# RWKV recurrence round four PSUM banks, and half of the first output columns projected beside it

## The chip, the cores and the metric

One core of a Trainium2 chip runs the whole program in one launch. The metric is device time in microseconds (us). TensorE (PE, with its weight loads PEld) multiplies, VectorE (DVE), ScalarE (ACT) and GpSimd (POOL) do the elementwise work, and SyncE's queue (SP) issues nearly all transfers. TensorE writes its results into PSUM, of which the program holds eight tiles of 128x512 fp32 at a time, called banks below.

## The reference

Two transformer blocks on a sequence of 512 tokens of width 1024 in fp32: the first has a hybrid token mixer, a cross attention on a memory of 256 tokens and a gated feed-forward, the second three attention branches. The change lies in the mixer of the first block, which joins an mLSTM (512 columns) with an RWKV-7 recurrence (512 columns) and projects both with one matrix:

```
hm = mlstm_chunkwise(q, k, v, i_pre, f_pre)             # 4 heads of 128
y_m = sigmoid(o) * standardize_heads(hm) * m_norm_g     # columns 0 to 511

def step(state, inp):                                   # RWKV: 8 heads of 64, 512 steps
    r_t, w_t, k_t, v_t, kk_t, a_t = inp
    sk = einsum('bhvk,bhk->bhv', state, kk_t)
    state = (state * w_t[:, :, None, :]
             - sk[..., None] * (kk_t * a_t)[:, :, None, :]
             + v_t[..., None] * k_t[:, :, None, :])
    y = einsum('bhvk,bhk->bhv', state, r_t)
yr = standardize_heads(yr) * r_gn_g + r_gn_b + (sum(rr * kr * r_rk) * vr)
y_r = yr * g                                            # columns 512 to 1023

x = x + concatenate([y_m, y_r], -1) @ w_out             # 1024 x 1024
```

## The kernel before

Activations lie transposed, features on partitions and the 512 tokens along a row. A dense product of fp32 precision is three matmuls for each 128x128 weight tile: high part of the weight by high part of the input, high by low, low by high. `unit` loads 128x512 fp32 of weights (`wraw`), ScalarE rounds it to the high part (`whi`), VectorE subtracts to get the low part (`wlo`); three buffers hold each of the two. One tile of one weight unit, three matmuls of 128x512, is called a unit step below.

The stage around the change is a merge of two streams that is written out as generators. `woven` advances the stream whose fraction of work done is smaller; `steps(n, ...)` counts a stream's yields in n-ths. The first stream is `rwkv_chain`: the recurrence in eight groups g of 64 tokens, each with two chunks of 32. For each group it does

- `columns(g)`: transposes of `BK` and of the values `xT` into two banks, evacuated into `St` (ScalarE) and `Z` (ScalarE, VectorE);
- `sides(g)`: transposes of `KR`, and products of `Z` and `Gm`, two banks, evacuated into `rgu`;
- `solve(g)`: `rgu` by the inverse `TT`, one bank, evacuated into `Z`;
- `ops(g)`: products of `St` and `Z`, two banks, which VectorE adds to `DR` and writes to `St` (four instructions);
- `step(g, c)`, c = 0 and 1: the recurrence itself, `Z` by `St`, two banks, which give the next `Z` and a piece of the output, in `sg` or `yt`.

`columns` and `sides` run two groups ahead of `step`, `solve` and `ops` one. After each second group, `rwkv_out` takes a block of 128 tokens through group normalisation (VectorE), transposes, gain and bias (ScalarE) and the gate into `xT[:, 4:8]`; it makes its yields between those of the chain. The second stream is `mlstm`, with the heads' projections (into the banks `mm`), their attention (into the banks `q`) and at the end `mem_kv`, the keys and values of the cross attention. The order of TensorE's instructions is the program order of this merge (`PIN`); those of the other engines are ordered by a scheduler with priorities, weights first.

After the merge `mixer_out` multiplies by `w_out` in two halves of the contraction: q = 0 takes the mLSTM's four tiles of 128 features, split into high and low parts in the room of `KR`; q = 1 takes the RWKV's four, in the room of `Gm`. The first OE = 4 output tiles m open four banks (`early`) and do their half q = 0 first; then each m in turn is finished with its half q = 1, and `x` (in the room of `BK`) is transposed and added.

The eight banks are `mm` (2), `p` (2), `q` (2), `s` (1) and `y` (1). `pt()` without a tag takes the next of `self.turns`. In this stage `turns` is `["p"]`: every tile of `columns`, `sides`, `solve`, `ops` and `rwkv_out` goes to one of the two `p` banks, and `step` names `s` and `y`.

Of the kernel before, what the change touches and what calls it, by code (L numbers as in the profile page):

```python
# [9 lines left out]
F32R = mybir.dt.float32r  # L10
# [6 lines left out]
S = 512  # L17
D = 1024
NB = S // 128
# [10 lines left out]
PS, LS, CS, XS = 16, 75, 90, 188  # L30
RW = "tile"
GS = 31
OE = 4
MY = 2
# [42 lines left out]
def weave(*gens):  # L77
    for _ in woven(*gens):
        pass
# [20 lines left out]
class Build:  # L100
# [378 lines left out]
    def mixer(self, yT, hpool, kept):  # L479
        nc, i = self.nc, self.i  # L480
        hh, hl = self.halves()
        h = (hh, hl)
        tc = self.tc
        self.turns, self.mms = ["p", "q"], ["mm", "mm", "s"]
        with self.tc.tile_pool(name="st", bufs=1, reuse_waits=RW) as st:
            self.basics()
            vectors = self.vectors(st)
            next(vectors)
            self.start(st, yT, kept, hh, hl)
            next(vectors)  # L490
            self.masks(hpool, st)
        v = self.vec
        with tc.tile_pool(name="rk", bufs=1, reuse_waits=RW) as rk:
            KR = self.tile(rk, [128, 4, 8, 4, 32], "KR", 1)
            BK = self.tile(rk, [128, 4, 8, 4, 32], "BK", 1)
            VT = yT[:, 4:8, :]
            PC = rk.tile([128, 4, 16], F32, name="PC")
            xt = hpool.tile([128, 512], F32, name="xt")
            yt = hpool.tile([128, 512], F32, name="yt")
            nc.gpsimd.memset(yt, 0.0)  # L500
            Gm = self.tile(rk, [128, 2, 8, 4, 64], "Gm", 1)
            small = hpool.tile([128, 64], F32, name="rsmall")
            omu = self.omu = small[:, 0:15]
            self.ts(omu, v["r_mu"], -1.0, 1.0)
            w0h, a0h, kah, kah1 = (small[:, 16 + 4 * q:20 + 4 * q] for q in range(4))
            self.ts(w0h, v["r_w0"], 0.5)
            self.ts(a0h, v["r_a0"], 0.5)
            self.ts(kah, v["r_ka"], 0.5)
            self.ts(kah1, v["r_ka"], -0.5, 1.0)
            rk2 = small[:, 32:40].rearrange("p (j e) -> p j e", e=2)  # L510
            bonus = hpool.tile([128, 32], F32, name="bonus")
            for j in range(4):
                self.ts(rk2[:, j], self.hsel, v["r_rk"][:, j:j + 1])
            TT = hpool.tile([128, 32, 32], F32, name="TT")
            rwu = TT[:, 0:16].rearrange("p a b -> p (a b)")
            nc.gpsimd.dma_start(rwu[0:64], i["r_w_up"][0])
            nc.gpsimd.dma_start(rwu[64:128], i["r_a_up"][0])
            rgu = hpool.tile([128, 512], F32, name="rgu")
            nc.gpsimd.dma_start(rgu, i["r_g_up"][0, 0:128])
            nc.gpsimd.dma_start(xt[0:32], i["r_g_up"][0, 128:160])  # L520
            sg = hpool.tile([128, 512], F32, name="sg")
            gb = hpool.tile([128, 1], F32, name="gb")
            self.rw = dict(sg=sg, gb=gb, KR=KR, BK=BK, VT=VT, PC=PC, Gm=Gm, rk=rk, rgu=rgu, rwu=rwu, xt=xt, yt=yt, rk2=rk2, bonus=bonus)
            with tc.tile_pool(name="ml", bufs=1, reuse_waits=RW) as ml:
                lstm = self.mlstm(ml, h, yT, hpool, kept)
                with tc.tile_pool(name="prep", bufs=1, reuse_waits=RW) as pr:
                    self.rwkv_prep(pr, h, small)
                    for _ in part(lstm, PS):
                        pass
                self.turns, self.mms = ["p"], ["mm"]  # L530
                with tc.tile_pool(name="mid", bufs=1, reuse_waits=RW) as mid:
                    self.rw["G"] = mid.tile([128, 4, S], F32, name="G")
                    with tc.tile_pool(name="inv", bufs=1, reuse_waits=RW) as iv:
                        self.pinned = PIN[0]
                        gates = self.gates(ml, iv)
                        next(gates)
                        weave(self.rwkv_inv(iv, TT), steps(LS + 5, part(lstm, 12), gates, part(lstm, GS), self.gate_rows(iv),
                                                           part(lstm, LS - 12 - GS)))
                    with tc.tile_pool(name="chain", bufs=1, reuse_waits=RW) as ch:
                        self.pinned = PIN[1]  # L540
                        weave(steps(CS, self.rwkv_chain(ch, TT, yT)), steps(XS + MY - LS - PS, lstm))
                self.pinned = ""
                self.turns, self.mms = ["p"], ["mm", "mm", "q", "q"]
                self.mixer_out(yT, rk, ml)
# [172 lines left out]
    def rwkv_chain(self, ch, TT, yT):  # L717
# [3 lines left out]
        nc, R = self.nc, self.rw  # L721
# [101 lines left out]
        def step(g, c):  # L823
            z, st = made[g]
            ix = 2 * g + c
            yn = ys[ix // 4 % 2].rearrange("p (j e k) -> p j e k", j=4, e=2)
            qs = slice(32 * (ix % 4), 32 * (ix % 4) + 32)
            for q in range(2):
                p = self.pt("sy"[q])
                pv = p[0:96, 0:256].rearrange("p (j e k) -> p j e k", j=2, e=2)  # L830
                js = slice(2 * q, 2 * q + 2)
                for j in range(2):
                    for e in range(2):
                        self.mm(pv[:, j, e], st[c][:, 2 * q + j, e], z[c][:, 2 * q + j, e, 0:64])
                for dst, src in ([(Z[(ix + 1) // 2 % 2][1 - c][CS[c], js, :, 0:64], pv[0:64])] if ix < 15 else []) + [(yn[qs, js], pv[64:96])]:
                    if q:
                        nc.vector.tensor_copy(dst, src)
                    else:
                        self.act(dst, src)
# [3 lines left out]
        def main():  # L843

            def rest(n):
                for _ in range(n):
                    yield 0

            consts(0)
            columns(0)  # L850
            yield from rest(2)
            sides(0)
            yield from rest(2)
            solve(0)
            columns(1)
            yield from rest(2)
            ops(0)
            consts(1)
            sides(1)
            yield from rest(2)  # L860
            for g in range(8):
                step(g, 0)
                yield from rest(1)
                if g < 7:
                    solve(g + 1)
                yield from rest(2)
                step(g, 1)
                if g % 2:
                    lates.append(self.rwkv_out(ys[g // 2 % 2], g // 2, yT))
                yield from rest(1)  # L870
                if g < 7:
                    ops(g + 1)
                    yield from rest(2)
                if g < 6:
                    consts(g + 2)
                    columns(g + 2)
                    yield from rest(2)
                    sides(g + 2)
                    yield from rest(2)


# [362 lines left out]
                nc.sync.dma_start(kept["v"].rearrange("p (s d) -> p s d", s=2)[:, s2, cc], t)  # L1244


    def mixer_out(self, xT, rk, ml):
        nc, i = self.nc, self.i
        x = self.tile(rk, [128, NB, D], "BK", 1)
        y = [self.tile(rk, [128, 2, 4, S], tag, 1, F32R) for tag in ("KR", "Gm")]  # L1250
        for q in range(2):
            for k in range(4):
                self.split_from(y[q][:, 0, k], y[q][:, 1, k], xT[:, 4 * q + k])
            if q == 0:
                for b in range(NB):
                    nc.sync.dma_start(x[:, b], i["x"][0, 128 * b:128 * b + 128, :])

        def half(ps, m, q):
            wu = self.unit(i["w_out"][0][512 * q:512 * q + 512, 128 * m:128 * m + 128], 4, 128)
            self.dense(ps, wu, (y[q][:, 0], y[q][:, 1]), range(4), q == 0, q == 1)  # L1260

        early = [self.pm() for _ in range(OE)]
        for m, ps in enumerate(early):
            half(ps, m, 0)
        for m in range(KD):
            if m < OE:
                ps = early[m]
            else:
                ps = self.pm()
                half(ps, m, 0)  # L1270
            half(ps, m, 1)
            p = self.pt()
            for b in range(NB):
                self.tr(p[:, 128 * b:128 * b + 128], x[:, b, 128 * m:128 * m + 128])
            xs = self.tile(ml, [128, 512], "k2", 2)
            self.act(xs, p)
            self.add(xT[:, m], xs, ps)
# [835 lines left out]
```

## Time and profile before

| | |
|---|---|
| median of three runs | 1573.21 us (1572.8 to 1574.99) |
| the profiled execution, its own time | 1564.84 us |
| its span, first to last instruction | 1563.1 us |
| PE busy, share of the span | 1523.2 us, 97% |
| DVE busy | 1087.7 us, 70% |
| ACT busy | 749.3 us, 48% |
| the merged stage of this change in it | about 248 to 400 us |
| `mixer_out` | about 416 to 464 us |

Busy is the time in which an engine had an instruction in work; idle time of an engine in the profile's rows is put down to what released it. A matmul's row shows its whole latency, and matmuls overlap, so the pace of a chain of them is read from the stretch and the count.

### The profile page before, as it was taken

The numbers are of one execution on the slowest core, as the hardware profiler recorded it, in microseconds if no ns is written. First come the engines' busy times: TensorE is split into PE (matmuls) and PEld (weight loads), VectorE is DVE, ScalarE is ACT, GpSimd is POOL, SyncE is SP. The second block draws the span as 40 slices with busy tenths as digits, with TensorE's granted clock in tenths as the row PEclk, the third lists the DMA queues.
The fourth block names the chain that finished last, engine by engine and source line by source line (L and its number), as shares of the span: only waits on it lengthen the run. The fifth ranks groups of instructions, "written<-read, shape, count | busy, mean of one in ns | idle before, by whom it ended". The sixth has DMA issues, their size and how long they took to land.

```text
span 1563.1 us, 23743 instructions
## 1 busy us (share of the span) xinstructions
PE 1523.2 (97%) x8487; PEld 1234.9 (79%) x8487; DVE 1087.7 (70%) x2536; ACT 749.3 (48%) x1469; POOL 101.0 (6%) x241
## 2 busy tenths in 40 slices
PE   6999999999999999999999999999999999999999
PEld 5777787788788888888888888888877778777787
DVE  7776697889757565534544578879998758765563
ACT  5645555456455444433432444456554445543431
POOL 7000402121000000000000001000000000000000
PEclk9999999999999999999999999999999999999999
DMA  7533122135534133333333334242322213224232
GB/s 249 142 72 81 48 64 53 39 92 147 170 93 131 41 94 92 97 96 100 95 97 99 92 105 106 65 117 77 90 62 66 70 52 85 77 65 128 62 96 100
DMA packets 209591, 144.85 MB, mean 93 GB/s; under 512 B 13492, under 2 KB 190787, under 8 KB 208960
## 3 DMA queue, kind: packets, MB, share of 16 engines
q1 hardware_dynamic: 208000, 141.66, 32.1%
q0 software_dynamic: 1280, 1.52, 0.4%
q8 instruction: 67, 1.10, 0.3%
q14 instruction: 52, 0.43, 0.1%
q10 hardware_dynamic: 192, 0.14, 0.0%
HBM read 134.90 MB, written 8.39 MB: 92 GB/s over the span
## 4 chain that ended last, share of the span: by engine, by line
PE 82%; DVE 10%; ACT 3%; DMA 2%; issue 2%; SPq 0%; DVEq 0%; ACTq 0%
PE mm L180 38%; PE q L180 27%; PE p L188 4%; PE p L191 3%; PE y L188 3%; DVE wlo L158 2%; PE s L188 2%; PE s L180 2%; PE q L188 2%; PE s L191 1%; PE q L191 1%; DVE St L158 1%; DVE lqk L158 1%; ACT whi L155 1%; DMA kvraw<-k_kept 1%
## 5 line engine op out<-in xcount | busy, mean ns | idle before, releaser
L155 ACT ACTIVATE whi<-wraw 128x512 fp32r<-128x512 f32 (+2 forms) x472 | 292.2, 621 | 499.6 <-PE mm L180 206.2
L158 DVE TENSOR_TENSOR wlo<-wraw,whi 128x512 fp32r<-128x512 f32 (+2 forms) x472 | 320.5, 680 | 187.9 <-ACT whi L155 180.3
L180 PE MATMUL mm<-hh,whi 128*128 128x512 f32 (+1 forms) x744 | 275.8, 387 | 1.3 <-DVE hh L158 1.3
L180 PE MATMUL mm<-hh,wlo 128*128 128x512 f32 (+1 forms) x680 | 261.6, 385 | 0.0
L180 PE MATMUL mm<-hl,whi 128*128 128x512 f32 x616 | 243.9, 396 | 0.0
L180 PEld LDWEIGHTS mm<-hh,whi 128*128 128x128 f32 x744 | 136.7, 190 | 27.4 <-issue 2.8
L180 PEld LDWEIGHTS mm<-hh,wlo 128*128 128x128 f32 x680 | 128.6, 189 | 24.1 <-issue 1.0
L180 PEld LDWEIGHTS mm<-hl,whi 128*128 128x128 f32 x616 | 116.2, 189 | 23.1 <-issue 2.6
L180 PE MATMUL q<-hh,whi 128*128 128x512 f32 x288 | 112.9, 392 | 0.0
L180 PE MATMUL q<-hl,whi 128*128 128x512 f32 x288 | 112.4, 390 | 0.0
L180 PE MATMUL q<-hh,wlo 128*128 128x512 f32 x288 | 112.4, 390 | 0.0
L180 PE MATMUL q<-whi,hh 128*128 128x512 f32 (+2 forms) x176 | 65.6, 385 | 0.0
L180 PE MATMUL mm<-whi,hh 128*128 128x512 f32 (+2 forms) x168 | 64.2, 389 | 0.0
L180 PEld LDWEIGHTS q<-hh,whi 128*128 128x128 f32 x288 | 54.1, 188 | 11.6 <-issue 0.7
L180 PEld LDWEIGHTS q<-hl,whi 128*128 128x128 f32 x288 | 54.1, 188 | 11.1 <-issue 0.2
L180 PEld LDWEIGHTS q<-hh,wlo 128*128 128x128 f32 x288 | 54.1, 188 | 11.1
L180 PE MATMUL q<-wlo,hh 128*128 128x512 f32 (+2 forms) x160 | 61.0, 381 | 0.0
L180 PE MATMUL mm<-wlo,hh 128*128 128x512 f32 (+2 forms) x152 | 58.4, 384 | 0.0
L180 PE MATMUL q<-whi,hl 128*128 128x512 f32 (+2 forms) x144 | 55.0, 382 | 0.0
L155 ACT ACTIVATE at_sm<-at_sm,at_mx 128x128 f32<-128x128 f32 (+3 forms) x64 | 35.7, 558 | 34.9 <-DVE at_mx L1567 34.3
L180 PE MATMUL mm<-whi,hl 128*128 128x512 f32 (+2 forms) x136 | 52.1, 383 | 0.0
L176 DVE SCALAR_TENSOR_TENSOR fy<-fc,vcols,fy 128x512 f32<-128x512 f32 x44 | 33.0, 752 | 8.9 <-ACT fy L155 8.1
(710 smaller groups left out, 3139.6 us busy)
## 6 DMA issues: line engine op xcount, KB each, us to landing
wraw<-in_w_in_dram SPq DMA_DIRECT2D x172, 256.0 KB, 2.9
wraw<-in_f_up_dram SPq DMA_DIRECT2D x88, 256.0 KB, 2.9
wraw<-in_f_down_dram SPq DMA_DIRECT2D x40, 256.0 KB, 2.8
wraw<-in_x_wkv_dram SPq DMA_DIRECT2D x32, 256.0 KB, 3.1
wraw<-in_w_out_dram SPq DMA_DIRECT2D x32, 256.0 KB, 2.8
wraw<-in_w_branch_dram SPq DMA_DIRECT2D x24, 256.0 KB, 2.7
wraw<-in_w_mem_kv_dram SPq DMA_DIRECT2D x16, 256.0 KB, 4.8
wraw<-in_x_wq_dram SPq DMA_DIRECT2D x16, 256.0 KB, 2.8
```

What stands on the lines that cost most here:

```text
L155: self.pin("a", self.nc.scalar.activation(out, in_, func, **kw))
L158: self.pin("v", self.nc.vector.tensor_tensor(out, a, b, op=op))
L176: self.pin("v", self.nc.vector.scalar_tensor_tensor(out, a, s, b, op0=op0, op1=op1))
L180: ins = self.nc.tensor.matmul(out, lhsT=a, rhs=b, start=start, stop=stop)
L188: self.pin("p", self.nc.tensor.matmul(out, lhsT=a, rhs=b, start=start, stop=stop))
L191: self.pin("p", self.nc.tensor.transpose(out, in_, self.ident if ident is None else ident))
```

## The change

`turns` becomes `["p", "s", "p", "y"]` for this stage, and `step` asks for its banks without a tag, so that all tiles of the recurrence go round the four banks. The half q = 0 of the four early output tiles moves from `mixer_out` into a generator `mixer_early`, which follows `mlstm` in the second stream; that stream is counted in 115 parts instead of 99, against 90 of the recurrence as before. `mixer_out` begins with the splits of the RWKV's half.

```diff
@@ mixer
                         self.pinned = PIN[1]
-                        weave(steps(CS, self.rwkv_chain(ch, TT, yT)), steps(XS + MY - LS - PS, lstm))
+
+                        self.turns = ["p", "s", "p", "y"]
+                        weave(steps(CS, self.rwkv_chain(ch, TT, yT)), steps(XS + MY - LS - PS + 4 * OE, lstm, self.mixer_early(yT, rk)))
                 self.pinned = ""
@@ rwkv_chain, step
             for q in range(2):
-                p = self.pt("sy"[q])
+                p = self.pt()
@@ rwkv_chain, main
                     sides(g + 2)
+                    R["read"] = g == 5
                     yield from rest(2)
@@
-    def mixer_out(self, xT, rk, ml):
+    def mixer_early(self, xT, rk):
+
         nc, i = self.nc, self.i
+        while not self.rw.get("read"):
+            yield None
         x = self.tile(rk, [128, NB, D], "BK", 1)
-        y = [self.tile(rk, [128, 2, 4, S], tag, 1, F32R) for tag in ("KR", "Gm")]
-        for q in range(2):
+        y = [self.tile(rk, [128, 2, 4, S], "KR", 1, F32R), None]
+
+        def parts(q):
             for k in range(4):
                 self.split_from(y[q][:, 0, k], y[q][:, 1, k], xT[:, 4 * q + k])
...
+        def half(ps, m, q, ks=range(4)):
+            wu = self.unit(i["w_out"][0][512 * q + 128 * ks[0]:512 * q + 128 * ks[-1] + 128, 128 * m:128 * m + 128], len(ks), 128)
+            for k in ks:
+                self.dense(ps, {k: wu[k - ks[0]]}, (y[q][:, 0], y[q][:, 1]), (k,), q == 0 and k == 0, q == 1 and k == 3)
+                yield 0
+
+        parts(0)
+        for b in range(NB):
+            nc.sync.dma_start(x[:, b], i["x"][0, 128 * b:128 * b + 128, :])
+        self.mms = ["mm", "mm", "q", "q"]
         early = [self.pm() for _ in range(OE)]
+        self.outs = x, y, half, early
         for m, ps in enumerate(early):
-            half(ps, m, 0)
+            yield from half(ps, m, 0)
+        self.parts = parts
+
+    def mixer_out(self, xT, rk, ml):
+        x, y, half, early = self.outs
+        y[1] = self.tile(rk, [128, 2, 4, S], "Gm", 1, F32R)
+        self.parts(1)
         for m in range(KD):
...
```

How instructions stand, at three places. The first is TensorE's queue at `columns(7)` and `sides(7)`, the last of their kind, from the transposes of the values on (`mm` is `mem_kv`'s dense product; the number behind a bank's name counts tiles). Before:

```order
L191 MATMUL p_4488<-ident,xT 64x128 x4
L180 MATMUL mm_4501<-whi_4505,hh_3605 128x512
L180 MATMUL mm_4501<-wlo_4504,hh_3605 128x512
L180 MATMUL mm_4501<-whi_4505,hh_3605 128x512
L180 MATMUL mm_4502<-whi_4505,hh_3605 128x512
L180 MATMUL mm_4502<-wlo_4504,hh_3605 128x512
L180 MATMUL mm_4502<-whi_4505,hh_3605 128x512
L191 MATMUL p_4525<-ident,KR_608 128x128 x4
L188 MATMUL p_4530<-Z_2782,Gm_614 32x64
```

and in the changed kernel:

```order
L191 MATMUL y_4561<-ident,xT 64x128 x4
L180 MATMUL mm_4363<-whi_4542,hh_3528 128x512
L180 MATMUL mm_4363<-wlo_4541,hh_3528 128x512
L180 MATMUL mm_4363<-whi_4542,hh_3528 128x512
L180 MATMUL mm_4362<-whi_4577,hh_3528 128x512
L180 MATMUL mm_4362<-wlo_4576,hh_3528 128x512
L180 MATMUL mm_4362<-whi_4577,hh_3528 128x512
L180 MATMUL mm_4363<-whi_4577,hh_3528 128x512
L180 MATMUL mm_4363<-wlo_4576,hh_3528 128x512
L180 MATMUL mm_4363<-whi_4577,hh_3528 128x512
L191 MATMUL p_4597<-ident,KR_608 128x128 x4
L188 MATMUL s_4602<-Z_2782,Gm_614 32x64
```

The tiles now lie in `y`, `p` and `s` in turn, and three unit steps of dense work instead of two stand between the transposes of the values and those of `KR`.

The second place is TensorE's queue around the transposes of the last block of the recurrence's output (`yt`), after the last `step`. Before, the dense work there is `mem_kv`'s:

```order
L180 MATMUL q_4796<-whi_4875,hh_3605 128x512
L191 MATMUL p_4885<-ident,yt 128x128 x4
L180 MATMUL q_4795<-whi_4897,hh_3605 128x512
L180 MATMUL q_4795<-wlo_4896,hh_3605 128x512
L180 MATMUL q_4795<-whi_4897,hh_3605 128x512
L191 MATMUL p_4904<-ident,xt 128x128 x4
```

and in the changed kernel it is the early half of the output projection (`KR` is now the split mLSTM half):

```order
L180 MATMUL q_4923<-KR_4908,wlo_4982 128x512
L191 MATMUL y_4993<-ident,yt 128x128 x4
L180 MATMUL q_4923<-KR_4908,whi_4983 128x512 x2
L180 MATMUL q_4923<-KR_4908,wlo_4982 128x512
L191 MATMUL p_5006<-ident,xt 128x128 x4
```

Counted in this queue from the last `step`: before, 12 unit steps stand ahead of the transposes of `yt`, and 6 of `mem_kv` and then 16 of the early half behind them, until the first product with the RWKV's half; now 14 stand ahead of them (four of `mem_kv`, ten of the early half) and 6 of the early half behind them.

The third place is VectorE's queue in the normalisation of that last block (`gst`, `gag` are its statistics). Before:

```order
L158 TENSOR_TENSOR sg<-sg,xt 128x512
L158 TENSOR_TENSOR wlo_4850<-wraw_4849,whi_4851 128x512
L158 TENSOR_TENSOR xT<-sg,G 128x4x128
L899 BN_AGGR gag_4780<-gst_4779 128x2
L898 BN_STATS gst_4779<-yt 128x6
L158 TENSOR_TENSOR wlo_4862<-wraw_4861,whi_4863 128x512
L899 BN_AGGR gag_4780<-gst_4779 128x2
L898 BN_STATS gst_4779<-yt 128x6
L899 BN_AGGR gag_4780<-gst_4779 128x2
L158 TENSOR_TENSOR wlo_4874<-wraw_4873,whi_4875 128x512
L171 TENSOR_SCALAR gvar_4826<-gag_4780 128x8
L158 TENSOR_TENSOR yt<-yt,gag_4780 128x512
```

and in the changed kernel:

```order
L158 TENSOR_TENSOR sg<-sg,xt 128x512
L158 TENSOR_TENSOR wlo_4964<-wraw_4963,whi_4965 128x512
L158 TENSOR_TENSOR xT<-sg,G 128x4x128
L902 BN_AGGR gag_4872<-gst_4871 128x2 x2
L158 TENSOR_TENSOR wlo_4982<-wraw_4981,whi_4983 128x512
L171 TENSOR_SCALAR gvar_4934<-gag_4872 128x8
L158 TENSOR_TENSOR yt<-yt,gag_4872 128x512
```

From the last copy into `yt` to its multiplication by the inverse deviation, six subtractions of weights (`wlo`) stand between before and three now, since one unit of weights lasts for four unit steps of the output projection and for two of `mem_kv`.

## Rows read from the trace of the kernel before

**Rows 1.** The page: engines over the whole span (busy us, share, instructions).
```profile
PE 1523.2 (97%) x8487; PEld 1234.9 (79%) x8487; DVE 1087.7 (70%) x2536; ACT 749.3 (48%) x1469; POOL 101.0 (6%) x241
```

**Rows 2.** Stretches of the span: start:end, length, then busy us and instructions of PE, PEld, DVE, ACT, POOL; granted TensorE clock (1 is full); DMA share; GB/s.
```profile
248.00:400.00 152.00, 139.62 (x1579) 119.34 (x1578) 130.87 (x365) 83.74 (x172) 31.06 (x55) 0.98 0.30 85
400.00:427.70 27.70, 25.14 (x118) 20.36 (x117) 19.59 (x57) 14.80 (x30) 0.00 (x0) 1.00 0.70 201
427.70:464.00 36.30, 36.30 (x172) 29.49 (x171) 17.97 (x26) 16.80 (x26) 0.00 (x0) 1.00 0.29 86
300.00:320.00 20.00, 17.59 (x187) 13.86 (x188) 19.28 (x82) 10.85 (x23) 5.74 (x7) 1.00 0.14 40
340.00:380.00 40.00, 36.76 (x453) 33.65 (x452) 38.03 (x111) 23.43 (x51) 8.83 (x15) 1.00 0.34 94
...
316.00:321.00 5.00, 2.89 (x19) 2.01 (x18) 4.94 (x10) 4.90 (x9) 4.30 (x1) 1.00 0.24 69
278.00:282.00 4.00, 1.69 (x12) 1.05 (x11) 3.08 (x5) 1.81 (x3) 1.79 (x4) 1.00 0.00 0
```

**Rows 3.** Waits of PE from 248 to 400 us: engine, line and tile that waited, what it waited for, us in total, times, longest.
```profile
PE p L191 <- DVE St L158: 4.1, 7, 1.0
PE p L191 <- ACT St L155: 3.1, 3, 1.4
PE mm L180 <- DVE hh L158: 1.3, 1, 1.3
PE p L188 <- DVE Z L765: 1.1, 2, 0.8
PE p L188 <- ACT sg L155: 0.7, 1, 0.7
PE p L191 <- DVE rgu L792: 0.7, 1, 0.7
PE p L188 <- DVE St L158: 0.5, 1, 0.5
PE q L191 <- DVE Dm L173: 0.5, 1, 0.5
```

**Rows 4.** Order of time on PE: start us, us, line, operation, tiles, shapes, count, and in brackets the idle time before and its releaser. Two of the waits of the group above.
```profile
279.46 0.63 PE L191 MATMUL p<-ident,BK 128*128 128x128 f32 x4 [0.95 <-DVE St L158]
281.44 0.63 PE L191 MATMUL p<-ident,xT 128*64 128x128 f32 x4 [1.36 <-ACT St L155]
```

**Rows 5.** Groups of instructions by line, engine, tiles and shapes, 248 to 400 us: count, busy us, mean ns of one, idle before them.
```profile
L158 DVE TENSOR_TENSOR wlo<-wraw,whi 128x512 fp32r<-128x512 f32 x34 | 23.4, 689 | 2.2 <-ACT whi L155 2.0
L155 ACT ACTIVATE whi<-wraw 128x512 fp32r<-128x512 f32 x33 | 20.8, 629 | 21.1 <-PE mm L180 12.7 <-issue 5.1 <-ACT yt L155 1.2
L158 DVE TENSOR_TENSOR St<-p,DR 64x384 f32<-64x384 f32 x32 | 17.8, 555 | 2.0 <-PE p L188 1.0
L155 ACT ACTIVATE St<-p 64x512 f32<-64x512 f32 x16 | 9.5, 592 | 3.9 <-PE p L191 3.6
```

**Rows 6.** The chain that ended last, pieces in order of time (start us, us, what): twelve matmuls of 128x256 twice.
```profile
325.00 2.86 PE mm L180 x12
...
338.73 1.65 PE mm L180 x12
```

**Rows 7.** Finer stretches, columns as in the second group: the slow stretch.
```profile
320.00:322.00 2.00, 1.54 (x11) 1.24 (x10) 1.94 (x5) 1.13 (x2) 1.88 (x3) 0.77 0.70 203
322.00:324.00 2.00, 1.26 (x10) 0.85 (x12) 1.10 (x4) 1.64 (x5) 1.37 (x3) 0.50 0.97 265
324.00:326.00 2.00, 2.00 (x37) 1.83 (x38) 1.26 (x3) 1.00 (x3) 0.00 (x0) 0.50 0.25 72
326.00:328.00 2.00, 2.00 (x12) 2.00 (x12) 0.69 (x1) 0.63 (x1) 0.00 (x0) 0.52 0.00 0
```

**Rows 8.** Order of time on PE after the last `step` (columns as in the fourth group).
```profile
398.92 0.84 PE L188 MATMUL y<-Z,St 128*96 128x64 f32 x8
399.57 0.48 PE L180 MATMUL mm<-whi,hh 128*128 128x512 f32 x1
...
411.48 0.63 PE L191 MATMUL p<-ident,yt 128*128 128x128 f32 x4 [2.56 <-DVE gg L158]
411.87 0.48 PE L180 MATMUL q<-whi,hh 128*128 128x512 f32 x1
...
416.52 0.63 PE L180 MATMUL mm<-KR,whi 128*128 128x512 f32 x2
...
427.72 0.63 PE L180 MATMUL mm<-Gm,whi 128*128 128x512 f32 x2
```

**Rows 9.** The chain that ended last: 24 matmuls of 128x512 without a gap.
```profile
419.48 5.60 PE q L180 x24
```

**Rows 10.** Order of time on DVE and ACT: the last block from the last `step` to its split halves `Gm`.
```profile
400.22 0.42 DVE L837 COPY yt<-y 32x256 f32<-32x256 f32 x1
...
410.05 0.69 DVE L158 TENSOR_TENSOR wlo<-wraw,whi 128x512 fp32r<-128x512 f32 x1
410.65 0.68 DVE L158 TENSOR_TENSOR yt<-yt,rs_y 128x512 f32<-128x512 f32 x1
...
412.15 1.50 ACT L155 ACTIVATE yt<-p,vcols 128x128 f32<-128x128 f32 x4 [2.19 <-PE p L191]
416.02 0.63 ACT L155 ACTIVATE Gm<-xT 128x512 fp32r<-128x512 f32 x1
...
416.68 0.69 DVE L158 TENSOR_TENSOR Gm<-xT,Gm 128x512 fp32r<-128x512 f32 x1
...
418.69 1.90 DVE L158 TENSOR_TENSOR Gm<-xT,Gm 128x512 fp32r<-128x512 f32 x3 [0.31 <-ACT Gm L155]
```

More of the change, by code (lines that the diff above doesn't have):

```diff
@@ L1244, in mem_kv @@
                 nc.sync.dma_start(kept["v"].rearrange("p (s d) -> p s d", s=2)[:, s2, cc], t)
-    def mixer_out(self, xT, rk, ml):
+    def mixer_early(self, xT, rk):
         nc, i = self.nc, self.i
+        while not self.rw.get("read"):
+            yield None
         x = self.tile(rk, [128, NB, D], "BK", 1)
-        y = [self.tile(rk, [128, 2, 4, S], tag, 1, F32R) for tag in ("KR", "Gm")]
-        for q in range(2):
+        y = [self.tile(rk, [128, 2, 4, S], "KR", 1, F32R), None]
+        def parts(q):
             for k in range(4):
                 self.split_from(y[q][:, 0, k], y[q][:, 1, k], xT[:, 4 * q + k])
[L1254 to L1260, printed above, removed]
+        def half(ps, m, q, ks=range(4)):
[7 more added lines that the diff above has]
+        self.mms = ["mm", "mm", "q", "q"]
         early = [self.pm() for _ in range(OE)]
+        self.outs = x, y, half, early
         for m, ps in enumerate(early):
-            half(ps, m, 0)
+            yield from half(ps, m, 0)
[4 more added lines that the diff above has]
+        self.parts(1)
         for m in range(KD):
@@ L1269, in mixer_out @@
                 ps = self.pm()
-                half(ps, m, 0)
-            half(ps, m, 1)
+                for _ in half(ps, m, 0):
+                    pass
+            for _ in half(ps, m, 1):
+                pass
             p = self.pt()
```

## The prediction

> **What bounds the kernel now.** I read the page first: PE is busy 97% of the span [rows 1], so time can come only from PE's idle time, from its clock and from work that it need not do. The change removes no matmul, so the first two are left. The second view is the table of stretches. In the merged stage, 248 to 400 us, PE is busy 139.6 of 152.0 us, so it stands 12.4 us; from 400 to 427.7 us it is busy 25.1 of 27.7 us; from there to 464 us it never stands [rows 2]. Of some 40 us of idle time in the whole program this stage and its tail therefore hold 15, and the change touches both. The third view says what PE waited for. The sum of the listed waits is 12.0 us [rows 3], nearly all of the 12.4. I sort them by whether the waiting matmul needed the *data* or only the *bank*. Transposes of `BK`, `xT`, `KR`, `sg` and `yt` (the tile `p` at L191) read nothing that the releaser wrote; `St`, `sg` and `rgu` are what VectorE or ScalarE were taking out of the bank's former tile. So 4.1 + 3.1 + 0.7 us there, and 0.7 + 0.5 us for the products of `Z` and `Gm` that waited for `sg` and `St`, are waits for a bank: 9.1 us. The waits for `hh` (1.3, `mem_kv`'s input), `Z` (1.1) and `Dm` (0.5) are waits for data: 2.9 us. A typical pair: the transposes of `BK` stand 0.95 us until the four `St` additions of `ops` have read their two banks, and the next transposes, of `xT`, 1.36 us until ScalarE has read the bank of the first [rows 4].
>
> **The four banks.** In the order before, seven of the eleven tiles of a group share two banks, so a tile waits for the evacuation of a tile taken hardly two places ahead. Round four banks, the place ahead is about four back: `columns` takes the banks of `step(g, 1)`, `sides` those of `ops`, the next `step` those of `columns`, `ops` those of `step(g, 0)` and `solve`. The dearest evacuation is that of `ops`, four additions of 0.555 us, 2.2 us [rows 5]. Before, the tile that followed it came one or two unit steps later. Now the transposes of `KR` come behind both transposes of `columns` (some 0.4 us each, as from 411.48 to 411.87 us [rows 8]) and at least three unit steps. A unit step is three matmuls; 24 matmuls without a gap take 5.60 us [rows 9], so it is 0.70 us, and three make 2.1 us. With the 0.8 us of transposes that is 2.9 us of cover for 2.2 us. The two `St` copies of ScalarE, 2 x 0.592 us, with one `whi` of 0.629 us ahead, 1.8 us [rows 5], are covered by the same 2 to 3 us. So the 9.1 us of bank waits go, by my reckoning. What comes instead? PE arrives earlier at the next data, and VectorE is its supplier. In 300 to 320 and 340 to 380 us VectorE is busy 57.3 of 60 us while PE stands 5.65 us [rows 2]: VectorE can give up no more than 2.7 us there. But of PE's 5.65 us about 2.8 are the waits for data (`hh`, `Dm`, `Z`), which I leave standing anyway, and the rest just fits. The second stream also runs faster against the recurrence, 115 parts to 90 instead of 99 to 90, so each step of the recurrence has more dense work beside it and VectorE's work for the recurrence is spread thinner. I allow 1.1 us for new short waits: **minus 8.0 us**. The bounds are 0 (VectorE gives nothing) and minus 12.4 (all idle time goes).
>
> **The clock.** From about 321 to 328 us the granted clock is 0.50, the lower of the two levels, 1.2 GHz, against 2.4 [rows 7]. Twelve matmuls of 128x256 take 2.86 us there and 1.65 us later [rows 6]. PE was busy about 6 us at the lower level (5.3 in the three stretches at about 0.50, the rest before), and half of that is lost: 3.0 us. Just ahead, from 316 to 321 us, PE was busy 2.89 of 5 us [rows 2]: bank waits, then 1.3 us for `hh`, whose eight instructions sit on ScalarE and VectorE while `columns` and `rwkv_out` ask for the same engines and banks. In 278 to 282 us PE was idle even more, 2.3 of 4 us, and the clock stayed [rows 2], so the fall is a near thing. In the new order `mem_kv` begins between a `solve` (1.0 us of work that covers part of the splits) and a `step`, and no tile of `columns` stands there. I expect about 1.5 us of idle time there instead of 3, and take it that the clock stays up: **minus 3.0 us**, between minus 3.0 and 0.
>
> The row shows a clock that fell once in this stage with two banks for seven tiles. The Trainium skill ("TensorE: Matmul & The Clock Gate", section "A second HAM failure mode: psum-queue depth-cycling") tells of a kernel that cycled through PSUM banks in every iteration, whose PE idled shortly between groups of matmuls so often that the clock went up and down. By that rule the change would add such falls; by the rows above, idle time falls and the clock with it stays up. The case has its place among the rivals, priced from rows.
>
> **The projection that is moved.** The 48 matmuls of 128x512 of the early half, their four weight units, the eight splits and the four loads of `x` are the same as before; only their place changes: no cost of their own. What changes is the cover of the last block. Let t0 be the end of the last `step`, 399.57 us [rows 8]. Before, 12 unit steps and two groups of transposes (8.4 + 0.8 us) end at 408.8 us, `yt` is normalised at 411.3, and PE stands 2.56 us [rows 8, 10]; then 22 unit steps hide all that follows. Now 14 unit steps and the same transposes take 10.6 us. VectorE's way from the copy of `yt` to its scaling ended 11.8 us after t0; six `wlo` stood in it, and now three, each of which pushes the next instruction back 0.60 us (410.05 to 410.65 us [rows 10]). So `yt` is ready at t0 + 10.0, and the transposes don't wait. Behind them stand only 6 unit steps and the transposes of `xt`, 5.0 us, before the first product with `Gm`, at t0 + 15.6. The way from the transposes of `yt` to the first low part of `Gm` took 5.9 us (411.48 to 417.37), to the last 9.1 us (420.6) [rows 8, 10]. So the first is there at t0 + 16.5 and the last at t0 + 19.7, while PE asks for the first at 15.8 and for the last after three more unit steps and two groups of `x` transposes, at about 18.7. PE stands 1.0 us. What is late next is thus the split of the last block, no longer its normalisation. Net: 1.0 - 2.56 = **minus 1.6 us**, between minus 2.6 and 0 (if `yt` comes as late as before, 1.2 us at the transposes and 1.0 at `Gm`, minus 0.4). The loads of `x` are queued behind weights on SP as before, and `mixer_out` from its second half on has the same order, with no idle time to lose or win [rows 2].
>
> **Sum.** 8.0 + 3.0 + 1.6 = 12.6 us. The profiled execution's own time goes from 1564.84 to 1552.2 us. The runs shown have a median of 1573.21 us, 8.4 above it; I carry the difference over unchanged: 1573.2 - 12.6 = **1560.6 us**, with 1558 to 1563 as this case's own range.
>
> **Rivals.**
> - *The clock falls all the same.* For it: the wait for `hh` is for data and remains, and one fall came with 2.1 us of idle time in 5. Against it: 278 to 282 us. 1573.2 - 9.6 = 1563.6 us.
> - *VectorE takes the place of the banks.* PE gets past the transposes and stands at the next `solve`, `ops` or `step` for `rgu` or `Z`. For it: VectorE busy 95% in 60 us of the stage. Against it: VectorE idles 21.1 us in the stage, 18 of them outside those 60 us, and more than half of PE's idle time (6.7 of 12.4 us) lies outside them too [rows 2]. With 2 us won of the 12.4, the clock as it was and the tail as forecast: 1573.2 - 3.6 = 1569.6 us; with the tail as late as before too, about 1572, no change that can be told.
> - *More falls of the clock.* PE idles for short times after each group and the clock goes down more often. Each fall like that at 321 us costs 3.0 us; three in all instead of one, with 9.6 us won otherwise: 1573.2 - 9.6 + 6.0 = 1569.6 us. Against it: one fall in 12.4 us of idle time before. The section of the Trainium skill named above describes this case.
> - *The steps lose their own banks; slower.* `s` and `y` belonged to `step` alone, which never waited for a foreign reader. Now its first tile needs ScalarE to have left the bank of `columns`. ScalarE works in order; if a `step` finds one `whi` and one `St` ahead, 1.2 us, then 16 steps pay 19 us, all on the recurrence, and with 9.6 won: about 1583 us. It decides against the change from a wait of 0.8 us a step (16 x 0.8 = 12.8 = 9.6 + 3.1 and a little). Against it: between `columns` and the next `step` stand `sides` and at least four unit steps, 4 us, and ScalarE is busy only 84 of 152 us [rows 2].
>
> **How the numbers follow.** Forecast 0.46; clock falls all the same 0.24; VectorE in place of the banks 0.12, and 0.06 for no change at all; more falls 0.05; slower steps 0.07. The likeliest gives the time. A measurement of this kernel tells 0.2%, 3.1 us, from no change: faster is below 1570.1 us. The first two cases, most of the third and half of the fifth lie there: 0.82; no change 0.10; slower 0.08. The range reaches up to 1570 us (leaving out the slower steps and no change, 0.13) and down to 1557 us, where all 12.4 us would go with the clock (1573.2 - 12.4 - 3.0 - 1.6 = 1556.2 is the bound).
>
> **What would show it.** Right: in the changed kernel's stage the waits of PE for `St` at L191 are gone or below 2 us in total, the waits for `hh`, `Z` and `Dm` remain; no stretch at 0.50 between 300 and 340 us; no wait at the transposes of `yt`, a wait of about 1 us before or in the first products with `Gm`, which begin some 16 us after the last `step` and about 12 us earlier than at 427.7. Wrong: PE standing at `step` or `solve` for `Z` or `rgu`, VectorE busy over 95% throughout, or waits of 3 us and more for `Gm`.

## The result: 1550.4 us, 22.6 us less

The changed kernel took 1550.42 us in the median (1550.11 to 1552.6, four runs) against 1573.01 us (1566.05 to 1574.99, four runs of the kernel before, beside it and earlier): a ratio of 0.987, 95% interval 0.9845 to 0.9894, or 17 to 24 us less. The prediction was 1560.6 us with 1557 to 1570: the sign was right, the gain almost twice the 12.6 us forecast, and the time lies below the range. Over all 36 runs of the kernel before on record the median is 1571.3 us, and the gain against it 20.9 us.

The profiled execution has a span of 1550.8 us, 12.3 us less than before. Its page, first line (as [rows 1]):

```profile
PE 1523.7 (98%) x8487; PEld 1237.1 (80%) x8487; DVE 1085.6 (70%) x2536; ACT 748.9 (48%) x1469; POOL 100.1 (6%) x241
```

The instructions are as many as before and PE is busy for as long; what went is idle time, and in the changed stage a part of the time at the lower clock. The stretches, with the columns of [rows 2], the last two being the place of the lower clock:

```profile
248.00:400.00 152.00, 149.59 (x1635) 129.46 (x1633) 136.44 (x387) 90.89 (x186) 32.26 (x62) 0.99 0.35 102
400.00:427.70 27.70, 27.70 (x135) 22.40 (x135) 21.31 (x59) 15.34 (x30) 0.00 (x0) 1.00 0.50 153
...
310.00:312.00 2.00, 0.91 (x5) 0.71 (x6) 2.00 (x6) 1.83 (x4) 0.00 (x0) 0.92 0.27 76
312.00:314.00 2.00, 2.00 (x13) 2.00 (x12) 1.94 (x5) 0.00 (x0) 0.00 (x0) 0.50 0.77 230
```

PE stands 2.4 us of the 152 instead of 12.4, and not at all from 400 to 427.7 us, where it stood 2.56. All its waits from 248 to 400 us, with the columns of [rows 3]:

```profile
PE mm L180 <- DVE hh L158: 1.1, 1, 1.1
PE mm L180 <- ACT hh L155: 0.7, 1, 0.7
PE q L191 <- DVE Dm L173: 0.4, 2, 0.2
PE y L188 <- DVE Z L807: 0.3, 1, 0.3
```

No wait for a bank is left, only waits for data. One stretch at the lower clock is left too, and it starts right behind the two waits for `hh`, at 311.7 us: 3.4 us long, where before it was 6.8 [rows 7].

The tail in order of time, PE, then VectorE and one row of ScalarE (as [rows 8] and [rows 10]):

```profile
399.40 0.84 PE L188 MATMUL p<-Z,St 128*96 128x64 f32 x8
400.05 0.48 PE L180 MATMUL q<-whi,hh 128*128 128x512 f32 x1
...
410.79 0.60 PE L191 MATMUL y<-ident,yt 128*128 128x128 f32 x4
...
415.96 0.51 PE L180 MATMUL mm<-Gm,whi 128*128 128x512 f32 x1
416.31 0.60 PE L191 MATMUL p<-ident,BK 128*128 128x128 f32 x4
416.69 0.50 PE L180 MATMUL mm<-Gm,whi 128*128 128x512 f32 x1
417.02 0.40 PE L180 MATMUL mm<-Gm,wlo 128*128 128x512 f32 x1
...
419.17 0.63 PE L180 MATMUL mm<-Gm,whi 128*128 128x512 f32 x2
...
409.07 0.69 DVE L158 TENSOR_TENSOR yt<-yt,rs_y 128x512 f32<-128x512 f32 x1
...
415.94 0.69 DVE L158 TENSOR_TENSOR Gm<-xT,Gm 128x512 fp32r<-128x512 f32 x1 [0.70 <-ACT Gm L155]
...
417.15 1.89 DVE L158 TENSOR_TENSOR Gm<-xT,Gm 128x512 fp32r<-128x512 f32 x3
...
415.28 0.63 ACT L155 ACTIVATE Gm<-xT 128x512 fp32r<-128x512 f32 x1 [1.57 <-DVE xT L158]
```

With t0 at 400.05 us, `yt` is scaled at t0 + 9.7 and its transposes run at t0 + 10.7 without a wait. The first product with `Gm` runs at t0 + 15.9; the low half of `Gm` is there at t0 + 16.6, and PE asks for it no earlier, because the first transposes of `x` (`BK`) stand between the first product, which takes the high half, and the next. The last low half is there at t0 + 19.0; its product, the second of the two from 419.17 us on, comes at about t0 + 19.4.

### The profile page after: what moved, and what is told of

It is laid out like the page before. It is cut to its first block, busy times and chain, and to the rows that moved or that the text cites. A ratio compares the mean times of both kernels' runs of the same rounds, so it can differ in the third digit from the quotient of the medians.

```text
span 1550.8 us, 23746 instructions
## 1 busy us (share of the span) xinstructions
PE 1523.7 (98%) x8487; PEld 1237.1 (80%) x8487; DVE 1085.6 (70%) x2536; ACT 748.9 (48%) x1469; POOL 100.1 (6%) x241
## 4 chain that ended last, share of the span: by engine, by line
PE 86%; DVE 9%; ACT 2%; issue 1%; DMA 1%; DVEq 0%; ACTq 0%
PE mm L180 39%; PE q L180 28%; PE p L188 4%; PE p L191 3%; PE y L188 3%; PE s L188 2%; DVE wlo L158 2%; PE s L180 2%; PE q L188 2%; PE s L191 1%; PE q L191 1%; DVE lqk L158 1%; DVE rs_t L158 0%; DVE m L1782 0%; DVE s L158 0%
## 5 line engine op out<-in xcount | busy, mean ns | idle before, releaser
L180 PEld LDWEIGHTS q<-hh,whi 128*128 128x128 f32 x288 | 54.1, 188 | 11.6 <-issue 0.7
```

What stands on the lines that cost most here:

```text
L180: ins = self.nc.tensor.matmul(out, lhsT=a, rhs=b, start=start, stop=stop)
```

## The experiments

To compare stages rather than spans, two marks bound the stage in every trace: the start of ScalarE's copy `mc`, ahead of the merge and the same instruction in all kernels, and the last product of `mixer_out` with `Gm`. Before, in its first trace:

```profile
231.59 0.58 ACT L155 ACTIVATE mc<-mm 128x512 f32<-128x512 f32 x1
464.15 0.39 PE L180 MATMUL mm<-Gm,wlo 128*128 128x512 f32 x1
```

and after:

```profile
234.82 0.58 ACT L155 ACTIVATE mc<-mm 128x512 f32<-128x512 f32 x1
452.62 0.39 PE L180 MATMUL mm<-Gm,wlo 128*128 128x512 f32 x1
```

That is 232.6 us before and 217.8 after, 14.8 us less; the span hides 3.2 of it, since this execution of the changed kernel reached the first mark later: ahead of it, where the code is the same, it has 17.1 us of stretches at a granted clock of 0.50, the first trace of before 10.2, and half of the difference is 3.4 us. All kernels, in us (idle: of PE, 248 to 400 and 400 to 430 us together; slow: the length of the stretches at a granted clock of 0.50 within the stage; left over: stage less idle less half of slow):

| kernel | timed, ratio to before | stage | idle | slow | left over |
|---|---|---|---|---|---|
| before, first and second trace | | 232.6, 232.5 | 15.0 | 6.8 | 214.2 |
| before, third to fifth trace | | 235.8 (each) | 14.9 | 13.7 | 214.1 |
| four banks alone | 1559.8, 0.993 | 225.2 | 9.1 | 3.4 | 214.4 |
| moved half alone | 1562.7, 0.995 | 228.8 | 12.6 | 3.4 | 214.5 |
| both, old pace | 1557.8, 0.992 | 225.0 | 9.1 | 3.4 | 214.2 |
| three banks | 1553.0, 0.989 | 219.2 | 6.0 | 0 | 213.2 |
| `MY` = 4 | 1558.4, 0.991 | 221.4 | 4.8 | 6.8 | 213.2 |
| after, first trace | 1550.4, 0.987 | 217.8 | 2.4 | 3.4 | 213.7 |
| after, second trace | | 216.6 | 2.7 | 0 | 213.9 |

The last column is within 214 ± 0.8 us in all twelve traces: idle time of PE and half of the slow stretches account for the stage, and nothing else is needed to explain its length.

### The four banks alone

```diff
 # kernel before
+self.turns = ["p", "s", "p", "y"]
 weave(steps(CS, self.rwkv_chain(ch, TT, yT)), ...
-                p = self.pt("sy"[q])
+                p = self.pt()
```

> The kernel before with one part of the change: the recurrence goes round the four banks, steps included; the output projection and the pace of the two streams stay as before. Theory A (the waits of TensorE for banks in the merged stage are the whole gain, and its tail costs about as much as before): the waits for St at L191 (7.2 us before) fall below 1 us, idle time of PE from 248 to 400 us falls from 12.4 to 2 to 4 us, the wait of 2.6 us for the last block stays, and the time is 8 to 13 us under that of the kernel before in the trace. Theory B (the moved projection and the slower pace of the recurrence take the waits away, the banks alone don't): idle time stays above 8 us and the gain is under 4 us. Theory C (idle time of PE brings further time at the lower clock in runs without a profile): the timed gain is larger than the traced one by 5 us or more.

Measured: ratio 0.9929 (0.9909 to 0.9949), 11 us less. Stretches and PE's waits, the last from the tail:

```profile
248.00:400.00 152.00, 144.23 (x1612) 124.86 (x1611) 137.05 (x399) 88.64 (x184) 34.74 (x62) 0.99 0.32 91
400.00:430.00 30.00, 28.64 (x133) 23.17 (x132) 18.81 (x42) 15.36 (x28) 0.00 (x0) 1.00 0.64 184
...
PE p L188 <- DVE Z L766: 1.5, 1, 1.5
PE s L191 <- DVE sg L158: 1.4, 1, 1.4
PE mm L180 <- DVE hh L158: 1.4, 1, 1.4
PE s L188 <- DVE Z L766: 1.3, 2, 0.8
PE mm L180 <- ACT hh L155: 0.8, 1, 0.8
PE p L188 <- DVE Z L806: 0.4, 1, 0.4
...
PE y L191 <- DVE yt L158: 1.4, 1, 1.4
```

The waits for `St`, 7.7 us before, are gone, but idle time falls by 4.6 us only, to 7.8: PE comes earlier to the next data and stands there for `Z` (3.2), `hh` (2.2) and `sg` (1.4, here the input of the transposes). This is the rival "VectorE takes the place of the banks", in part. Theory A had expected 2 to 4 us of idle time and theory B a gain under 4 us; both missed. The timed gain is 6.2 us larger than the 5.0 us between the two profiled executions (1564.84 and 1559.87), as theory C had it; the further traces of before, below, show why.

### The moved half alone

```diff
 # changed kernel
-self.turns = ["p", "s", "p", "y"]
+self.turns = ["p"]
-                p = self.pt()
+                p = self.pt("sy"[q])
```

> The changed kernel with the banks as before: two p banks for the recurrence, s and y for its steps; the early half of the output projection stays beside the recurrence, in 115 parts. Theory A: the waits for St at L191 stay at 5 to 8 us, only the wait for the last block (2.6 us) goes, gain 0 to 4 us. Theory B: idle time from 248 to 400 us falls below 5 us, gain 8 us or more. Theory C: the timed runs vary from run to run by several us as those of the kernel before did (1566 to 1575), with a lower mean clock in the longer ones.

Measured: ratio 0.9951 (0.9934 to 0.9969), 8 us less.

```profile
248.00:400.00 152.00, 139.41 (x1560) 119.07 (x1560) 126.68 (x355) 85.59 (x175) 28.32 (x56) 0.99 0.33 95
400.00:430.00 30.00, 30.00 (x171) 24.72 (x167) 24.51 (x71) 16.22 (x32) 0.00 (x0) 1.00 0.49 148
366.00:368.00 2.00, 2.00 (x12) 2.00 (x11) 0.69 (x1) 0.54 (x2) 0.70 (x3) 0.52 0.25 74
...
PE p L191 <- ACT St L155: 4.0, 3, 1.4
PE p L191 <- DVE St L158: 2.5, 3, 1.0
```

The bank waits stay, with 12.6 us of idle time in all, in spite of the new pace: without the banks it does nothing for them. The tail's wait of 2.56 us is gone, and so is the stretch at 0.50 near 321 us, though PE waits for `hh` and for banks ahead of it here too; a shorter one, 3.4 us from 366.1 us on, stands behind bank waits instead. Theory A holds for the waits, but the gain is more than its 0 to 4 us; of theory C it holds that the three runs of 1565 us have clocks of 0.992 and 0.993, those below 1562 us 0.995 and 0.996. The stage is 3.8 us shorter than in before's first trace and 7.0 shorter than in three others, on which more below.

### Both, at the old pace

```diff
-steps(XS + MY - LS - PS + 4 * OE, lstm, self.mixer_early(yT, rk))
+steps(XS + MY - LS - PS, lstm, self.mixer_early(yT, rk))
```

> The changed kernel with the second stream counted in 99 parts again, so that it advances against the recurrence as before; the four banks and the moved half stay. Theory A (the pace carries the gain of the moved half in the stage: with more dense work beside each step the data of the recurrence come in time): the waits of the bank experiment come back, for Z, sg and hh at products, TensorE idle 7 to 8 of 152 us from 248 to 400 us, no wait in the tail since all of the early half then stands behind the last step; 1556 to 1559 us. Theory B (the four banks alone free the stage, the waits there are chance of the order): idle 2 to 4 us and 1550 to 1553 us. Theory C (the pace matters to the clock through the tail alone): time as theory A but a granted clock of 0.995 and above.

Measured: ratio 0.9924 (0.991 to 0.9939), 11.6 us less.

```profile
248.00:400.00 152.00, 144.24 (x1611) 125.20 (x1610) 137.38 (x391) 88.83 (x183) 32.14 (x56) 0.99 0.31 92
...
PE p L188 <- DVE Z L767: 1.5, 1, 1.5
PE s L191 <- DVE sg L158: 1.4, 1, 1.4
...
PE y L191 <- DVE yt L158: 1.3, 1, 1.3
```

Row for row this is the kernel with the banks alone, the tail's wait for `yt` too, which theory A had not expected: with as much dense work ahead of it as before, the last block comes too late just the same. So moving the projection is worth nothing measurable beside the banks at the old pace; the count of 115 instead of 99 is worth 7.2 us of the stage (225.0 to 217.8). With more dense work beside each step of the recurrence, VectorE has its data ready in time, and the 7.8 us of idle time become 2.4, the tail's 1.3 us none.

### Three banks

```diff
-self.turns = ["p", "s", "p", "y"]
+self.turns = ["p", "s", "p"]
```

> The changed kernel with three banks for the recurrence instead of four (the two p banks and s in turn p, s, p; y is left unused). Theory A (waits fall with the distance at which a bank is used again): idle time of PE from 248 to 400 us between that of the changed kernel (2.4 us) and that with the banks as before (12.6 us), 4 to 8 us, time 1553 to 1560 us. Theory B' (what counts is that steps have no banks of their own and all tiles share): as the changed kernel within 1 us of idle time. If the steps suffered from sharing, waits of PE at p or s L188 for Z or St would show, 16 times.

Measured: 1552.99 us (1550.91 to 1557.3), ratio 0.9889 (0.987 to 0.9908).

```profile
248.00:400.00 152.00, 145.99 (x1631) 126.47 (x1630) 135.30 (x383) 89.37 (x183) 28.61 (x55) 1.00 0.35 102
...
PE p L188 <- DVE Z L807: 2.4, 3, 1.0
```

The idle time of 6.0 us is what theory A had expected, but only in part for its reason: waits for banks come back for 1.3 us only (`sg` 0.8, at the one `step` that waits for a bank, and `St` 0.5). The largest is for `Z` from L807, 2.4 us: the products of `ops` wait for the data of `solve`. The stage's 219.2 us are 1.4 to 2.6 more than with four: the third bank brings most of it, and the two kernels' intervals overlap.

### More room ahead of `mem_kv`

```diff
-MY = 2
+MY = 4
```

Two more rests of the second stream ahead of `mem_kv`, so that the splits of its input `hh` have more time: the one wait of the changed kernel that seemed worth removing.

> The changed kernel with MY = 4 instead of 2: two more places of the recurrence between the splits of mem_kv's input (hh) and its first matmul. In the trace of the changed kernel PE waits there 1.8 us for hh, and the clock is at 0.50 for the 3.4 us behind it. Theory C: without the wait the fall goes too, 1.8 + 1.7 = up to 3.5 us faster than the changed kernel, 1547 to 1549 us. Rival (the fall has nothing to do with the wait): 1.8 us faster at most, the stretch at 0.50 near 312 us stays. Rival (the wait only moves): the same time as the changed kernel, 1550 us.

Measured: 1558.36 us (1553.85 to 1560.2), ratio 0.991 (0.9895 to 0.9926), about 8 us slower than the changed kernel (6 us by the ratios to the runs of before beside each). All that was expected of it missed.

```profile
314.00:316.00 2.00, 0.51 (x6) 0.26 (x5) 1.93 (x6) 1.34 (x3) 0.75 (x1) 1.00 0.97 279
...
318.00:320.00 2.00, 2.00 (x17) 1.78 (x16) 1.81 (x7) 0.30 (x1) 0.00 (x0) 0.50 0.03 9
...
PE y L188 <- ACT Z L155: 1.5, 1, 1.5
PE s L188 <- DVE Z L767: 1.4, 2, 1.2
PE p L188 <- DVE Z L767: 1.2, 1, 1.2
```

The waits for `hh` are gone, but the steps of the recurrence now follow one another with less dense work between them, and PE stands for `Z`: 4.8 us idle instead of 2.4. Behind the longest of these waits, which ends at 315.96 us, the clock is at 0.50 for 6.8 us instead of 3.4. Together that is 4.1 us; the stage grew by 3.6 to 4.8. Four of its five runs had a mean clock of 0.991 or 0.992, those of the changed kernel 0.993 to 0.997. In its trace one slow stretch more, 3.4 us from 12.8 us on, lies ahead of the first mark, where the code is the same; what else makes up the 6 to 8 us is open.

### More traces of both kernels, unchanged

> The kernel before once more, unchanged, for a trace of an execution of some 1570 us, which most of its executions take, beside the one of 1564.8 us that the prediction used. Theory C (the time between 1563 and 1573 us is lower clock): the trace has five or more stretches of 3.4 us at 0.50 more than the first trace's, at a span of 1569 us or more; they lie in the merged stage, 248 to 430 us, behind PE's waits for banks; PE's idle time is the same within 1 us. Rival (they lie elsewhere, before 248 or behind 430 us, where the change does nothing): then the change can't have taken them away. Rival (the clock is as in the first trace, and transfers or waits are longer): PE's idle time grows by the difference.

> As the run before this one, a second draw: theory C expects the stretches at 0.50 at about the same places of the merged stage, since the waits that precede them are fixed by the order of the instructions; a span under 1566 us should show at most two of them there.

> The kernel before once more, unchanged, for the places of its stretches at the lower clock. Theory (what the runs lose to the clock lies behind waits that the change removes): beside the two early stretches and the one at 321 us, further ones between 360 and 420 us when the mean clock is 0.991 or below, none when it is 0.994; 1564 to 1574 us. Rival (the clock falls elsewhere, away from the stage): the additional stretches lie before 248 or behind 430 us.

> The kernel before a last time, unchanged; expectations as for the fourth look: with a mean clock of 0.991 or below further stretches at the lower clock between 360 and 420 us, or, by the rival, away from the stage.

> The changed kernel once more, unchanged. Theory: no stretch at the lower clock between 330 and 430 us, at most the one behind the wait for hh at 312 us; clock 0.993 to 0.997, 1549 to 1553 us. Rival (its clock varies as that of the kernel before does): stretches at new places and a time over 1555 us.

Before took 1567.55, 1569.2, 1572.07 and 1572.34 us in these traces, the second to the fifth, at mean clocks of 0.995, 0.991, 0.991 and 0.991; after 1547.52 us at 0.996, a little below the 1549 to 1553 us expected. PE's waits for banks are the same in all five traces of before (`St` 4.1 and 3.0 to 3.1 us). But in the three at 0.991 there are two stretches at 0.50 more in the stage, 3.4 us each, which the first two traces do not have; theory C had expected five or more. In the fourth trace (4.5 us later at the first mark than the first), stretches and then PE in order of time:

```profile
370.00:372.00 2.00, 1.76 (x8) 1.76 (x9) 1.87 (x8) 1.69 (x5) 0.00 (x0) 0.56 0.49 136
...
418.00:420.00 2.00, 2.00 (x9) 1.60 (x8) 0.00 (x0) 1.51 (x4) 0.00 (x0) 0.51 1.00 277
...
367.96 0.65 PE L188 MATMUL p<-Z,Gm 32*32 32x64 f32 x32 [0.76 <-DVE Z L765]
370.24 1.11 PE L191 MATMUL p<-ident,yt 128*128 128x128 f32 x4 [0.73 <-DVE rgu L792]
...
417.58 0.66 PE L191 MATMUL p<-ident,yt 128*128 128x128 f32 x4 [2.56 <-DVE gg L158]
...
236.05 0.58 ACT L155 ACTIVATE mc<-mm 128x512 f32<-128x512 f32 x1
471.84 0.40 PE L180 MATMUL mm<-Gm,wlo 128*128 128x512 f32 x1
```

The first lies behind waits for `Z` and a bank (`rgu`), the second right behind the tail's 2.56 us. Half of 2 x 3.4 us is 3.4; the stage is 235.8 us in all three, 3.2 more than in the first trace. In the changed kernel these waits are gone, and neither of its two traces has a stretch there. Of all twelve traces, a stretch that starts between 365 and 371 us is found in four of the six with two banks for the recurrence and in none of the six with more; one from 413 to 418 us on in three of the five with the tail's wait of 2.56 us and in none of the seven without it. So the theory fits the two stretches, but the waits alone don't bring them, since the first two traces have the waits and no stretch. For the rival (the clock falls elsewhere) there is one, ahead of the first mark, which is 3.4 us long in two of the traces of before and 6.8 in three, and varies in the other kernels too.

The first mark differs by the clock as well. At the start of the program, where all kernels have the same instructions, the first trace of before (first row) has ten dense matmuls in 2 us, the fourth six:

```profile
14.00:16.00 2.00, 2.00 (x10) 1.67 (x9) 2.00 (x5) 2.00 (x4) 1.99 (x5) 1.00 1.06 355
14.00:16.00 2.00, 2.00 (x6) 1.57 (x5) 1.59 (x4) 0.76 (x4) 1.95 (x6) 1.00 1.05 332
```

They follow one another every 0.43 us instead of every 0.23, up to 18.6 us; 0.43 us is also their pace in the stretch at 0.50 behind the tail's wait (from 418.46 to 418.89 us). The second row says 1.00, because the first record of the clock comes after it in that trace, and so the mean clock leaves this start out. By 23.0 us the fourth trace is 3.1 us behind the first, 2.7 of it since the first dense matmul. The second and fifth traces of before and the one with `MY` = 4 start in this way too, for a shorter time; the eight others don't. The first mark comes between 231.5 and 236.3 us in the twelve traces; less PE's idle time ahead of it, half of the stretches at 0.50 and half of PE's busy time ahead of the first record of the clock, 207.8 to 209.0 us remain in all of them.

Of 32 runs of before timed beside the experiments, 19 had a mean clock of 0.989 to 0.991 (median 1572.2 us) and 13 one of 0.993 to 0.995 (median 1568.9). The clock of the three traces with the two stretches is thus the more frequent one, and the first trace showed the other.

## Why the prediction was wrong

**The step that failed is the last of the sum: "I carry the difference over unchanged."** The median of before stood 8.4 us above its profiled execution, and I took these as something that the change does not touch. Of the changed kernel the median stands 2.2 us below its profiled execution (1550.4 against 1552.6). That execution had been forecast at 1552.2 us, so up to there the sum came out, with luck: the stage became 14.8 us shorter instead of 12.6, and the first mark came 3.2 us later. Nor can the sizes of the terms alone explain the miss: with each at its bound (12.4, 3.0 and 2.6 us) the time would be 1555.2 us.

What the 8.4 us are made of shows in the fourth trace (1572.07 us, 7.2 above the first): 4.5 us lie ahead of the first mark (236.05 against 231.59), 3.2 us are the two slow stretches in the stage, and behind it the trace is 0.5 us shorter. The 3.2 us come with waits that the change removes, and in no trace without these waits. The 4.5 us lie where both kernels have the same instructions: 2.7 of them are the slow start, and the stretch near 192 us is 6.8 us long instead of 3.4.

**Each term of the sum was also too small.** Measured on the trace after, against the same first trace:

- *Four banks*, forecast -8.0: idle time fell by 10.0 us. The sorting was right: the bank waits went, all 9.1 us, and of the data waits `hh` and `Dm` remained, 2.2 us; those for `Z` (1.1) went. Of the 1.1 us allowed for new waits 0.5 us came at `hh` (1.8 instead of 1.3) and 0.3 at `Z` from L807, and 0.4 us of unlisted idle time went too. The reason that I gave for so few new waits, the pace, holds: without it 5.4 us of them come. It was written as an aside, though it carries more of the gain than the moved work itself.
- *Clock*, forecast -3.0 (0.46, against 0.24 for the clock falling all the same): the stretch shrank from 6.8 to 3.4 us in one trace (-1.7) and is missing in the other (-3.4). So the sign "no stretch at 0.50 between 300 and 340 us" failed in the first and held in the second, in two executions of one program with the same waits for `hh`. What decides between them no run shows, so a hit with the 3.0 us would have been luck.
- *Tail*, forecast -1.6: -2.56. The first times were right (10.7 forecast as 10.6 for the transposes of `yt`, 16.6 forecast as 16.5 for the first low half). The 1.0 us of new wait, which was for the last low half, did not come, from both sides: it was there at t0 + 19.0 instead of 19.7, and PE asked for it at about 19.4 instead of 18.7. For the first low half PE did not stand either: the first product needs only the high half, which ScalarE had done at 415.91 us, and 0.4 us of transposes of `x` come next.

These make 14.3 us for the first trace of after (stage: 14.8) and, with its 2.7 us of idle time, 15.6 for the second (stage: 15.9 to 16.0), where I had 12.6. Against the third to fifth traces of before the stage is 18.0 to 19.2 us shorter, which is within the measured 17 to 24. Up to the difference of the medians, 3 to 5 us remain, 2 to 3 against the median of all 36 runs of before. About 1 us lies behind the stage; the clock ahead of the first mark can make up the rest, but which of the timed runs started slowly no trace shows, so this part stays open.

**The rivals.** *VectorE takes the place of the banks* is what the banks alone do, in part; the pace keeps it away (VectorE is busy 136.4 of 152 us after, more than the 130.9 before, and PE waits 1.8 us for it). *More falls of the clock* did not come: the stage has 0 to 3.4 us of slow stretches instead of 6.8 to 13.7. The rule of the Trainium skill that I had put beside it ("TensorE: Matmul & The Clock Gate", section "A second HAM failure mode: psum-queue depth-cycling") is not borne out here, since going round more banks took PE's idle time away. What does hold is a rule of the Trainium skill in "Perfetto Trace Analysis", section "Optimizing Tensor Performance": independent groups should rotate through different banks so that evacuations lie beside matmuls; the trace agrees, with 12.4 us of idle time down to 7.8 by that alone. *The steps lose their own banks* did not come: the list of waits after holds none of a `step` for a bank (the one for `Z` from L807 is at the products of `ops`).

## What to carry to other kernels

Before a profiled execution's distance to the median is carried through a change, ask what it is made of: at another mean clock the stage that is changed may have slow stretches that this one trace does not show, and the start may be slow without the mean clock telling; a second trace tells. When banks are added, a part of the waits turns into waits for data; giving the recurrence more independent work per step is what collects the rest. A matmul group that is split into high and low halves needs them one after the other, so check which half the first product asks for.

## What the runs showed of the hardware

- One program with the same waits takes one of two patterns of the granted clock: in two traces one stretch at 0.50 in the stage, in three traces three, at the same places of the program. Why one or the other comes is open.
- The sum of idle time does not set it: 6.0 us idle in the stage with three banks and no slow stretch, 4.8 us with `MY` = 4 and one of 6.8 us. The same two waits for `hh`, 1.8 us, are followed by 3.4 us at 0.50 in one trace of the changed kernel and by none in the other, nor with three banks.
- A slow stretch of 3.4 or 6.8 us costs half its length: on that, and idle time, twelve traces agree within 0.8 us in 214.
- The start of the program is at the lower pace for a varying time: in four of twelve traces the first dense matmuls come every 0.43 us instead of every 0.23, for up to 18.6 us after the start of the program, and the mean granted clock counts this in one of the four only (0.995 in both of before's first two traces, the second of which is 2.7 us longer).
